# Layer 1's projections cut into half tiles and placed at the end of the attention rounds, their evacuation and splits one round later

## The chip, the cores and the metric

The kernel runs on one core of one Trainium2 chip. The metric is the device time of one execution in microseconds. Five engines work side by side: PE (matmuls), DVE (vector), ACT (activations, copies), POOL (GpSimd) and SP, which issues the transfers. Each has its own queue of instructions and waits for the others by semaphores.

## The reference

A two-layer transformer on 256 latent and 256 context tokens of width 1024, all in float32. Layer 0 mixes by window and latent attention, layer 1, the last, by differential attention of the latent tokens over all 512 tokens; each is followed by a mixture of experts (32 experts, two per token). The change touches layer 1's mixer:

```
h = modulate(rmsnorm(x), shift, scale)              # latent 256 x 1024, context 256 x 1024
q, k, v = split(h @ w_in, (1024, 1024, 1024))        # 8 heads; q, k: 2 x 64 each, v: 128
q1, q2, k1, k2 = rope(...)                           # of the latent tokens
lam = exp(lq1 . lk1) - exp(lq2 . lk2) + lambda_init
o = softmax(q1 k1' / 8) v - lam * softmax(q2 k2' / 8) v
x_lat = x_lat + gate * (rmsnorm(o, subln) * (1 - lambda_init)) @ w_out
```

## The kernel before

The program is recorded in the order in which it is written (manual_schedule, line 128), and each engine keeps that order. SBUF holds 24 buffers of 1 MB (S(), line 136), shared by data ("data") and by weights on their way ("w"). All weights come as a stream of 1 MB tiles in the order of plan(): emit() issues the next one on SP, pump() does so while fewer than 24 - max(budget, data) buffers hold weights, and budget(n) sets that bound. The expert weights of layer 1 follow behind layer 1's other weights in the same stream.

Matmuls that need more than single fp32r accuracy are done in three: mm3 (line 396) multiplies hi x hi, hi x lo and lo x hi. So each weight tile is split into hi and lo first: Splits.step (line 410) splits one half of 128 columns, a copy to hi on ACT or on another engine and a subtraction to lo, by default on DVE; get() hands out a finished tile and makes the next one, both halves.

w_in of layer 1 has 12 tiles of 256 columns: numbers 0 to 3 are q, 4 to 7 k, 8 to 11 v, in the order DWO. After the first (k, through proj_step) a loop runs the 11 others: k_tile and q_tile make two blocks of 128 rows of 24 matmuls each, of 512 columns for k (all tokens) and of 256 for q; v_tile makes two pieces of 48 matmuls of 256 columns, which read both halves of the tile. A q or k block is evacuated by rope_lat on DVE (line 565: one product, four products of 32 rows, one sum) and split again, hi on ACT and lo on POOL; a v piece is copied by ACT.

Then run_units goes through 16 units (8 heads x 2 blocks of 128 queries). Round i has, in this order: d_scores (6 matmuls) and d_max (DVE) of unit i + 2, the hook early1(i), d_pv of unit i - 1, a fill (a step of the modulation projections, 4 matmuls) in some rounds, d_scale (DVE) of unit i + 1, d_transpose of unit i (PE, copy on ACT), d_exp of unit i + 2 (ACT). The hook also splits half tiles of w_out in rounds 7, 9, 11 and 13, with both steps on POOL. Behind the rounds stand the turns of the outputs, the output projection (out_block) and the MoE of layer 1.

PSUM has four banks of tag A (scores), three of tag B (pieces, transposes, d_pv) and one of tag C (fills).

Of the kernel before, what the change touches and what calls it, by code (L numbers as in the profile page):

```python
# [19 lines left out]
P = 128  # L20
# [28 lines left out]

ADL = 3  # L50

DWO = (4, 5, 6, 8, 0, 7, 9, 1, 10, 2, 11, 3)
ADO = {0: (0, 1), 1: (2, 3, 4), 2: (5,), 3: (6,), 4: (7,)}

# [61 lines left out]
def model_kernel(ctx: ExitStack, tc: tile.TileContext, xin, small, cst, ada0, adaw, win, wuq, wukv, wout0, dwin,  # L116
# [24 lines left out]
    def free(n):  # L141
        st_["data"] -= n
# [41 lines left out]
    def U(shape=(512,), dt=F32):  # L184
        return up.tile([P] + list(shape), dt, tag="u", name="u")
# [7 lines left out]
    def psB():  # L193
        return psb.tile([P, 512], F32, tag="B", name="psB")
# [268 lines left out]
    def xc(c):  # L463
        return xmap[c]
# [44 lines left out]
    def h_lo(l, c, xa, hi, lo, gp=False):  # L509
        for s in range(2):  # L510
            hs, b = HALF[s], modT[:, l, 0, c, s:s + 1]
            if s and gp:
                GP.tensor_scalar(xa[:, hs], xa[:, hs], b, None, op0=ALU.add)
                GP.tensor_tensor(lo[:, hs], xa[:, hs], hi[:, hs].bitcast(F32), ALU.subtract)
            else:
                DVE.scalar_tensor_tensor(out=lo[:, hs], in0=xa[:, hs], scalar=b, in1=hi[:, hs].bitcast(F32),
                                         op0=ALU.add, op1=ALU.subtract)
# [44 lines left out]
    DVE.tensor_copy(UB, csv("U"))  # L562


    def rope_lat(ps, dst, p0, cosn, sinn):

        t = U((SEQ,))
        r = U((SEQ,))
        DVE.tensor_tensor(t[p0:P], ps[p0:P, 0:SEQ], csv(cosn)[p0:P], ALU.mult)
        for q in range(p0 // 32, 4):  # L570
            a, b = slice(32 * q, 32 * q + 32), slice(32 * (q ^ 1), 32 * (q ^ 1) + 32)
            DVE.tensor_tensor(r[b], ps[a, 0:SEQ], csv(sinn)[a], ALU.mult)  # L572
        DVE.tensor_tensor(dst[p0:P, 0:SEQ], t[p0:P], r[p0:P], ALU.add)
# [221 lines left out]
    def run_units(units, scores, maxs, exps, scale, transpose, pv, fills, hook, prime=0, ex=None):  # L795

        n = len(units)
        mx, pts, PT = {}, {}, {}
        if ex is None:
            ex = {}  # L800
            for i in range(2):
                ex[i] = exps(units[i], *maxs(units[i], scores(units[i])))
        fill(prime)
        pts[0] = scale(units[0], ex.pop(0))
        for i in range(n - 1):
            if i + 2 < n:
# [855 lines left out]
    for c in range(KC):  # L1662
# [13 lines left out]
    DVE.tensor_scalar(nlam, lamt[:, 2:3], -LAMBDA_INIT, None, op0=ALU.add)  # L1676
    k1 = [[S((4, NTOK), F32R) for _ in range(2)] for _ in range(2)]

    def k_out(j, ps):
        dst = U()  # L1680
        ACT.copy(dst[:, SEQ:], ps[:, SEQ:])
        rope_lat(ps, dst, 0, "cosA", "sinA")
        split(*(x[j // 4].v[:, j % 4, :] for x in k1), dst, GP)

    def k_tile(j2):
        ws = W1.get()
        for j in range(2):
            ps = psB()
            s = slice(j * P, (j + 1) * P)
            mm3(ps, KC, lambda k: (ws[0][:, k, s], ws[1][:, k, s]), h13)  # L1690
            k_out(2 * j2 + j, ps)
        free(2)

    def q_tile(j2):
        ws = W1.get()
        for j in range(2):
            ps = psB()
            s = slice(j * P, (j + 1) * P)
            mm3(ps[:, 0:SEQ], KC, lambda k: (ws[0][:, k, s], ws[1][:, k, s]),
                lambda k: tuple(x[:, 0:SEQ] for x in h13(k)))  # L1700
            dst = U((SEQ,))
            rope_lat(ps, dst, 0, "cosA", "sinA")
            split(*(x.v[:, 2 * j2 + j, :] for x in q1), dst, GP)
        free(2)

    def v_tile(j):
        ws = W1.get()
        for t2 in range(2):
            ps = psB()
            for t in range(2):  # L1710
                ts_ = slice((2 * t2 + t) * P, (2 * t2 + t + 1) * P)
                mm3(ps[:, t * 256:(t + 1) * 256], KC, lambda k: tuple(x[:, ts_] for x in h13(k)),
                    lambda k: (ws[0][:, k, :], ws[1][:, k, :]))
            ACT.copy(v1[j // 2].v[:, 2 * t2:2 * t2 + 2, (j % 2) * 256:(j % 2 + 1) * 256],
                     ps.rearrange("p (t n) -> p t n", t=2))
        free(2)

    wl = [W1.get(False)]
    pss = [psA() for _ in range(2)]
# [5 lines left out]
    free(2)  # L1725
    q1 = [S((KC, SEQ), F32R) for _ in range(2)]
    v1 = [S((4, 512)), S((4, 512))]
    budget(18)
    for j in DWO[1:]:
        (q_tile, k_tile, v_tile)[j // 4](j % 4)  # L1730
    free(4)
    oD = S((16, P))
    budget(11)

    def d_scores(u):
        h, qt = u
        ps = [psA(), psA()]
        for a, b in ((0, 0), (0, 1), (1, 0)):
            for i in range(2):
                pr = slice(64 * i, 64 * i + 64)  # L1740
                PE.matmul(ps[i], q1[a].v[pr, h, qt * P:(qt + 1) * P], k1[b][h // 4].v[pr, h % 4, :],
                          start=(a + b == 0), stop=(a == 1))
        return ps

    def d_max(u, ps):
        st = T((8,))
        for i in range(2):
            DVE.tensor_reduce(out=st[:, i:i + 1], in_=ps[i], axis=AX.X, op=ALU.max)  # L1748
        DVE.tensor_scalar(st[:, 2:4], st[:, 0:2], -0.125, None, op0=ALU.mult)
        return ps, st  # L1750
# [29 lines left out]
    def d_pv(u, PTs):  # L1780
        h, qt = u
        PT, rec = PTs
        ps = psB()
        for b in range(4):
            PE.matmul(ps[:, 0:P], PT[:, b * P:(b + 1) * P], v1[h // 4].v[:, b, (h % 4) * P:(h % 4 + 1) * P],
                      start=(b == 0), stop=(b == 3))
        sq = U((P,))
        ACT.activation(sq, ps[:, 0:P], AF.Square, scale=rec, accum_out=ssD[:, 0, 2 * h + qt:2 * h + qt + 1])
        DVE.tensor_scalar(oD.v[:, 2 * h + qt, :], ps[:, 0:P], rec, None, op0=ALU.mult)

# [18 lines left out]
        DVE.scalar_tensor_tensor(out=lo, in0=ps, scalar=sl1, in1=hi.bitcast(F32), op0=ALU.mult, op1=ALU.subtract)  # L1809

    def early1(i):
        if i in {2: 13, 10: 14}:
            budget({2: 13, 10: 14}[i])
        if i == 9:
            free(3)
            budget({2: 13, 10: 14}[10])
        if i in (7, 9, 11, 13):
            Wo.step(GP, GP)
        if i == 14:

            oDs.extend(S((KC, SEQ), F32R) for _ in range(2))
            d_rstd(0, 12)
        if i == 15:
            d_norm(0)
            d_norm(1)
            d_turn(0)
        if i == 16:
            d_norm(2)
            d_turn(1)

    run_units([(h, qt) for h in range(8) for qt in range(2)], d_scores, d_max, d_exp, d_scale, d_transpose, d_pv,
              lambda i: i in (1, 2, 3, 14, 15), early1, 3)
    d_rstd(12, 16)
    d_norm(3)
    d_turn(2)
# [196 lines left out]
```

## Time and profile before

| | us |
|---|---|
| runs: lowest, median, highest of three | 1467.99, 1470.62, 1471.46 |
| profiled execution, its own time | 1473.68 |
| its span, first to last instruction | 1471.9 |
| PE, DVE, ACT, POOL busy in the span | 1306.0, 578.9, 373.1, 139.6 |

The span is divided by what the program does: layer 1's projections begin with the first tile at 782 us, the other 11 run from 795.1 to 897.5, the attention rounds and their tail to 964.7, the output projection and the router to about 1017, and the MoE of layer 1 to the end. A matmul's end is modelled and neighbours overlap, so a busy PE is read together with the distance between starts.

### The profile page before, as it was taken

To read this page: it belongs to the slowest core of one execution; us is meant where nothing else is said; L and a number is where in the kernel's file an instruction comes from. 1 tells how busy PE (TensorE), PEld (TensorE's weight loads), DVE (VectorE), ACT (ScalarE), POOL (GpSimd) and SP (SyncE) were. 2 spreads that over 40 slices of the span, in tenths; PEclk is the share of its full clock that TensorE was granted. 3 is DMA by queue.
4 is the path that set the end of the run, shared out by engine and by line. 5 is a ranking of instruction groups with operands and counts; after the bars stand their busy time and mean duration, and the time that the engine had idled before them with its cause. 6 is when DMAs were issued, how large, how long until landed. Compare 5 with 4: busy or idle time off the path is not lost.

```text
span 1471.9 us, 21790 instructions
## 1 busy us (share of the span) xinstructions
PE 1306.0 (89%) x8439; PEld 720.9 (49%) x8439; DVE 578.9 (39%) x1423; ACT 373.1 (25%) x800; POOL 139.6 (9%) x129
## 2 busy tenths in 40 slices
PE   5998999989999989989889999797998786877867
PEld 3675668935435343525226896593432321323313
DVE  4577874464232313222237657945311110111102
ACT  4444654331111111101024334743110100101002
POOL 1112341210000000000013211211000000000000
PEclk9999999999999999999999999999999999999989
DMA  9834444489999999999998238356999999999995
GB/s 379 334 114 144 173 143 173 162 333 369 409 421 421 420 421 421 422 420 421 401 410 343 72 115 318 154 210 275 422 420 421 420 422 421 421 421 421 422 413 218
DMA packets 70076, 487.16 MB, mean 331 GB/s; under 512 B 7632, under 2 KB 7760, under 8 KB 13392
## 3 DMA queue, kind: packets, MB, share of 16 engines
q1 hardware_dynamic: 69968, 485.71, 81.2%
q8 instruction: 69, 1.13, 0.3%
q14 instruction: 39, 0.32, 0.1%
HBM read 484.63 MB, written 1.05 MB: 330 GB/s over the span
## 4 chain that ended last, share of the span: by engine, by line
DMA 26%; PE 16%; DVE 7%; ACT 2%; issue 1%; DVEq 0%; SPq 0%; ACTq 0%
DMA s<-in_ew_dram 26%; PE psA L1356 3%; PE psA L1388 2%; PE psB L402 2%; PE psB L403 2%; PE psB L401 2%; DVE t L1748 1%; DVE u L1766 1%; PE psA L401 1%; PE psA L402 1%; PE psA L403 1%; DVE s L394 1%; DVE u L572 0%; DVE t L1764 0%; DVE s L1398 0%
## 5 line engine op out<-in xcount | busy, mean ns | idle before, releaser
L1356 PE MATMUL psA<-s 128*32 128x512 f32 (+2 forms) x2336 | 420.9, 627 | 81.4 <-DMA s<-in_ew_dram 72.1
L1356 PEld LDWEIGHTS psA<-s 128*32 128x32 f32 (+2 forms) x2336 | 114.7, 122 | 364.2 <-issue 209.8
L1398 DVE SCALAR_TENSOR_TENSOR s<-psB,modT,s 128x256 f32<-128x256 f32 x296 | 120.4, 476 | 220.8 <-PE psB L1405 220.7
L1388 PE MATMUL psA<-s,u 128*32 128x512 f32 (+1 forms) x1168 | 186.9, 606 | 11.7 <-DMA s<-in_ew_dram 10.4
L1393 DVE SCALAR_TENSOR_TENSOR u<-psA,t,u 128x512 fp32r<-128x512 f32 x48 | 36.0, 750 | 232.5 <-ACT u L1392 232.5
L1388 PEld LDWEIGHTS psA<-s,u 128*32 128x32 f32 (+1 forms) x1168 | 54.5, 120 | 121.8 <-issue 95.2
L1405 PE MATMUL psB<-u 128*128 128x512 f32 (+1 forms) x384 | 95.8, 369 | 13.1 <-DVE s L1398 4.7
L1530 DVE TENSOR_TENSOR u<-u,psA 128x512 f32<-128x512 f32 x24 | 16.5, 688 | 221.6 <-PE psA L1356 221.6
L401 PE MATMUL psB<-s 128*128 128x256 f32 (+1 forms) x304 | 98.8, 325 | 0.2 <-DVE s L888 0.2
L402 PE MATMUL psB<-s 128*128 128x256 f32 (+1 forms) x304 | 98.1, 323 | 0.3 <-DVE s L394 0.3
L403 PE MATMUL psB<-s 128*128 128x256 f32 (+1 forms) x304 | 98.0, 322 | 0.0
L1382 ACT COPY u<-psB 128x512 f32<-128x512 f32 x24 | 14.1, 587 | 329.7 <-PE psB L1380 329.7
L1405 PEld LDWEIGHTS psB<-u 128*128 128x128 f32 x384 | 58.7, 188 | 72.4 <-issue 36.1
L1392 ACT ACTIVATE u<-psA,t 128x512 fp32r<-128x512 f32 x48 | 33.0, 688 | 176.6 <-PE psA L1388 171.1
L1527 ACT ACTIVATE u<-psA 128x512 f32<-128x512 f32 x24 | 14.4, 599 | 226.0 <-PE psA L1356 225.9
L1339 PE MATMUL psB<-s 128*128 128x256 f32 x544 | 68.0, 285 | 0.7 <-ACT u L1382 0.7
L394 DVE TENSOR_TENSOR s<-s 128x1024 fp32r<-128x1024 f32 (+3 forms) x56 | 51.6, 966 | 39.9 <-ACT s L391 39.9
L1339 PEld LDWEIGHTS psB<-s 128*128 128x128 f32 x544 | 65.9, 191 | 2.6 <-issue 1.6
L401 PEld LDWEIGHTS psB<-s 128*128 128x128 f32 x304 | 57.9, 190 | 8.4 <-issue 1.7
L402 PEld LDWEIGHTS psB<-s 128*128 128x128 f32 x304 | 57.9, 190 | 4.7 <-DVE s L394 0.6
L403 PEld LDWEIGHTS psB<-s 128*128 128x128 f32 x304 | 57.9, 190 | 4.5
L401 PE MATMUL psA<-s 128*128 128x256 f32 (+1 forms) x200 | 58.7, 294 | 0.0
(354 smaller groups left out, 1704.6 us busy)
## 6 DMA issues: line engine op xcount, KB each, us to landing
s<-in_ew_dram SPq DMA_DIRECT2D x376, 1024.0 KB, 19.8
s<-in_adaw_dram SPq DMA_DIRECT2D x40, 1024.0 KB, 6.8
s<-in_dwin_dram SPq DMA_DIRECT2D x12, 1024.0 KB, 9.8
s<-in_ada_dram SPq DMA_DIRECT2D x8, 1024.0 KB, 20.1
s<-in_wout_dram SPq DMA_DIRECT2D x8, 1024.0 KB, 8.3
s<-in_ew_dram SPq DMA_DIRECT2D x16, 512.0 KB, 15.3
s<-in_win_dram SPq DMA_DIRECT2D x5, 1024.0 KB, 21.1
s<-in_xin_dram SPq DMA_DIRECT2D x2, 1024.0 KB, 8.5
```

Of the source, the lines that this page charges most:

```text
L394: eng.tensor_tensor(lo, src, hi.bitcast(F32), ALU.subtract)
L401: PE.matmul(ps, lh, rh, start=(k == 0), stop=False)
L402: PE.matmul(ps, lh, rl, start=False, stop=False)
L403: PE.matmul(ps, ll, rh, start=False, stop=(k == n - 1))
L1339: PE.matmul(ps[:, i * n:(i + 1) * n], src(t, cs_(c0 + i)), oh[:, t, 0:n], start=(t == 0 and a == 0), stop=(t == T_ - 1 and a == 1))
L1356: PE.matmul(ps[sl, :], xg(hf * 4 + k, sl), wt(m, hf)[:, k, :], start=(hf == 0 and k == 0), stop=(hf == 1 and k == 3))
L1388: PE.matmul(ps[sl, :], ht[:, k, sl], wt(2, hf)[:, k, :], start=(k == 0), stop=(k == 3))
L1392: ACT.activation(yh, ps, AF.Copy, scale=gsl)
L1393: DVE.scalar_tensor_tensor(out=yl, in0=ps, scalar=gsl, in1=yh.bitcast(F32), op0=ALU.mult, op1=ALU.subtract)
L1398: DVE.scalar_tensor_tensor(out=xc(c)[:, HALF[s]], in0=ps[:, HALF[s]], scalar=modT[:, l, 5, c, s:s + 1], in1=xc(c)[:, HALF[s]], op0=ALU.mul ...
L1405: PE.matmul(ps[:, 0:nt], ysp[a][:, cs_(q)], oht[:, 0:nt], start=(a == 0), stop=(a == 1))
L1530: TT(hm, sl, pm[1], ALU.mult)
```

## The change

The tiles stand in another order (DWO; ADO holds the tiles of the modulation that go between them). The 11 tiles after the first are cut into 22 pieces, half a tile each. q_piece, k_piece and v_piece issue the matmuls at once and hand back two functions, one that evacuates and one that splits. Two pieces of q0 come ahead of everything, one of k1 behind the scores of each of the first two units, two of q1 ahead of round 0; the 16 others stand at the end of rounds, as PIECES lists. A round begins with evacs() (the pieces of the round before), and splits() stands behind its exponentials: per piece its split and, if no finished weight tile is there, one half of the next weight tile, with the subtraction on POOL. The temporaries of the rope and q's destination lie in the context halves of xT, which nothing reads any more. The three fills ahead of the rounds go into them, the splits of w_out go to rounds 12 to 15, and budget is 19 until round 9, where it was 18 and then 11.

```diff
-DWO = (4, 5, 6, 8, 0, 7, 9, 1, 10, 2, 11, 3)
+PIECES = {0: 2, 1: 1, 2: 1, 3: 1, 4: 2, 5: 2, 6: 1, 7: 1, 8: 2, 9: 1, 10: 1, 12: 1}
+DWO = (4, 0, 5, 1, 8, 9, 6, 2, 10, 7, 3, 11)
...
+    budget(19)
...
+    def q_piece(j2, j, ws):
+        ps = psB()
+        s = slice(j * P, (j + 1) * P)
+        mm3(ps[:, 0:SEQ], KC, lambda k: (ws[0][:, k, s], ws[1][:, k, s]),
+            lambda k: tuple(x[:, 0:SEQ] for x in h13(k)))
+        dst = room()
+        tr = (room(), room())
+        return (lambda: rope_lat(ps, dst, 0, "cosA", "sinA", tr),
+                lambda: split(*(x.v[:, 2 * j2 + j, :] for x in q1), dst, GP))
...
+    def piece(n=1):
+        for _ in range(n):
+            j, i = pieces.pop(0)
+            if i == 0:
+                cur.append(W1.get(False))
+            made.append((q_piece, k_piece, v_piece)[j // 4](j % 4, i, cur[0]))
...
+    def splits():
+        for n in range(len(made)):
+            made.pop(0)[1]()
+            if not W1.made:
+                W1.step(GP)
...
-    for j in DWO[1:]:
-        (q_tile, k_tile, v_tile)[j // 4](j % 4)
...
-    run_units([(h, qt) for h in range(8) for qt in range(2)], d_scores, d_max, d_exp, d_scale, d_transpose, d_pv,
-              lambda i: i in (1, 2, 3, 14, 15), early1, 3)
+    piece(2)
+    evacs()
+    splits()
+    for i in range(2):
+        mx1[i] = d_max(units[i], d_scores(units[i]))
+        piece()
+        ex1[i] = d_exp(units[i], *mx1.pop(i))
+    evacs()
+    pts1[0] = d_scale(units[0], ex1.pop(0))
+    splits()
+    piece(2)
+    for i in range(n_u + 1):
+        evacs()
+        if i + 2 < n_u:
+            mx1[i + 2] = d_max(units[i + 2], d_scores(units[i + 2]))
+        early1(i)
+        if 0 < i:
+            d_pv(units[i - 1], PT1.pop(i - 1))
+        if i in (2, 6, 11, 13, 14, 15):
+            fill()
+        if i + 1 < n_u:
+            pts1[i + 1] = d_scale(units[i + 1], ex1.pop(i + 1))
+        if i < n_u:
+            PT1[i] = d_transpose(units[i], pts1.pop(i))
+        if i + 2 < n_u:
+            ex1[i + 2] = d_exp(units[i + 2], *mx1.pop(i + 2))
+        splits()
+        if i in (12, 13, 14, 15):
+            Wo.step(GP, GP)
+        piece(PIECES.get(i, 0))
```

POOL from layer 1's norm (the first row) to the output weights, before. A subtraction of 128x512 or 128x256 is the split of a k or q block; 128x8x128 is half a weight tile.

```order
L514 TENSOR_TENSOR s<-u,s 128x256
L394 TENSOR_TENSOR s<-u,s 128x512 x6
L394 TENSOR_TENSOR s<-u,s 128x256 x2
L394 TENSOR_TENSOR s<-u,s 128x512 x2
L394 TENSOR_TENSOR s<-u,s 128x256 x6
L393 CAST s<-s 128x8x128
L394 TENSOR_TENSOR s<-s 128x8x128
```

The same place now, from the norm to the first of the long run of weight halves behind round 0:

```order
L516 TENSOR_TENSOR s<-u,s 128x256
L396 TENSOR_TENSOR s<-u,s 128x512 x2
L396 TENSOR_TENSOR s<-s 128x256
L396 TENSOR_TENSOR s<-s 128x8x128
L396 TENSOR_TENSOR s<-s 128x256
L396 TENSOR_TENSOR s<-s 128x8x128
L396 TENSOR_TENSOR s<-u,s 128x512
L396 TENSOR_TENSOR s<-s 128x8x128
L396 TENSOR_TENSOR s<-u,s 128x512
L396 TENSOR_TENSOR s<-s 128x8x128
L396 TENSOR_TENSOR s<-s 128x256
L396 TENSOR_TENSOR s<-s 128x8x128
```

Between the splits of the blocks POOL now has the weight halves: two of k1 (between q0's blocks), two of q1 (between k1's), two of v0 (between q1's), and so on, 18 in all.

ACT around the projection of k's third and v's first tile before, where L391 on u is the split of a block, L391 on s that of half a weight tile, and L1714 the copy of a v piece:

```order
L391 CAST s<-u 128x512
L391 CAST s<-s 128x8x128 x2
L1714 COPY s<-psB 128x2x256 x2
L391 CAST s<-s 128x8x128 x2
L391 CAST s<-u 128x256 x2
L391 CAST s<-s 128x8x128 x2
```

ACT in rounds 0 and 1 now (L1808 is the copy of the transposes, L1789 an exponential, L1728 the copy of a v piece, L1821 the square in d_pv, L393 a split):

```order
L1808 COPY u<-psB 128x512
L1789 ACTIVATE u,t<-psA,t 128x512 x2
L393 CAST s<-s 128x256
L393 CAST s<-s 128x8x128
L393 CAST s<-s 128x256
L393 CAST s<-s 128x8x128
L1728 COPY s<-psB 128x2x256 x2
L1821 ACTIVATE s,ssD<-psB,t 128x128
L1808 COPY u<-psB 128x512
L1789 ACTIVATE u,t<-psA,t 128x512 x2
L393 CAST s<-s 128x8x128 x2
```

The two casts of v0's weights stand behind the exponentials of round 0, and those of v1's behind the ones of round 1; PE has the pieces that read them at the end of the same rounds.

## Rows read from the trace of the kernel before

**Rows 1.** Busy time by stage: window, length, engines with instructions, PEclk, DMA share, GB/s

```profile
795.10:897.50 102.40, 102.09 (x721) 96.06 (x719) 63.66 (x112) 33.00 (x50) 14.81 (x14) 1.00 0.35 124
897.50:953.90 56.40, 47.41 (x326) 30.16 (x325) 53.08 (x114) 37.73 (x108) 15.75 (x10) 0.97 0.61 241
...
1000.00:1017.00 17.00, 10.26 (x51) 5.64 (x45) 11.72 (x43) 6.02 (x10) 3.65 (x4) 0.80 0.48 202
1017.00:1471.90 454.90, 369.59 (x2115) 139.03 (x2115) 77.91 (x217) 50.72 (x90) 1.90 (x1) 0.96 0.97 402
```

**Rows 2.** Order of time, PE, projections: start, length, line and operation

```profile
795.09 0.39 PE L401 MATMUL psB<-s 128*128 128x512 f32 x1
...
795.54 0.40 PE L403 MATMUL psB<-s 128*128 128x512 f32 x1
...
897.20 0.28 PE L402 MATMUL psB<-s 128*128 128x256 f32 x1
897.32 0.28 PE L403 MATMUL psB<-s 128*128 128x256 f32 x1
```

**Rows 3.** Order of time, PE, one attention round

```profile
939.44 0.63 PE L1773 MATMUL psB<-identR,u 128*128 128x128 f32 x4 [0.16 <-DVE u L1766]
940.00 0.96 PE L1741 MATMUL psA<-s 64*128 64x512 f32 x6
940.89 1.16 PE L1785 MATMUL psB<-s,u 128*128 128x128 f32 x8
```

**Rows 4.** Order of time, DVE: a rope, and the maxima of a round

```profile
799.81 0.42 DVE L569 TENSOR_TENSOR u<-psA,u 128x256 f32<-128x256 f32 x1 [1.00 <-ACT u L1681]
800.25 1.72 DVE L572 TENSOR_TENSOR u<-psA,u 32x256 f32<-32x256 f32 x4
802.00 0.42 DVE L573 TENSOR_TENSOR u<-u 128x256 f32<-128x256 f32 x1
...
939.21 1.28 DVE L1748 TENSOR_REDUCE t<-psA 128x1 f32<-128x512 f32 x2
```

**Rows 5.** Order of time, ACT: from an exponential to what follows the second

```profile
938.02 0.69 ACT L1756 ACTIVATE u<-psA,t 128x512 f32<-128x512 f32 x1
...
939.36 0.36 ACT L1788 ACTIVATE u<-psB,t 128x128 f32<-128x128 f32 x1
```

**Rows 6.** Groups by line, 796 to 898 us: busy, mean ns, idle before

```profile
L394 DVE TENSOR_TENSOR s<-s 128x1024 fp32r<-128x1024 f32 x21 | 25.8, 1267 | 25.2 <-ACT s L391 25.2
...
L391 ACT CAST s<-s 128x1024 fp32r<-128x1024 f32 x20 | 20.0, 1047 | 0.0
...
L394 POOL TENSOR_TENSOR s<-u,s 128x512 fp32r<-128x512 f32 x8 | 10.4, 1297 | 33.1 <-ACT s L391 33.1
...
L394 POOL TENSOR_TENSOR s<-u,s 128x256 fp32r<-128x256 f32 x7 | 5.2, 740 | 56.3 <-ACT s L391 56.3
L391 ACT CAST s<-u 128x512 fp32r<-128x512 f32 x8 | 5.0, 620 | 27.2 <-DVE u L573 23.4 <-issue 3.8
...
L391 ACT CAST s<-u 128x256 fp32r<-128x256 f32 x7 | 2.8, 406 | 24.1 <-DVE u L573 24.1
```

**Rows 7.** Order of time, DVE and POOL: one operation alone, and beside a weight half

```profile
903.56 0.22 DVE L1764 SCALAR_TENSOR_TENSOR t<-t,nlam 128x1 f32<-128x1 f32 x1
...
916.02 2.42 DVE L1764 SCALAR_TENSOR_TENSOR t<-t,nlam 128x1 f32<-128x1 f32 x1
...
916.06 2.37 POOL L394 TENSOR_TENSOR s<-s 128x1024 fp32r<-128x1024 f32 x1 [2.60 <-PE psC L323]
```

**Rows 8.** Order of time, PE, the round behind its longest wait

```profile
926.31 0.88 PE L1773 MATMUL psB<-identR,u 128*128 128x128 f32 x4 [3.66 <-DVE u L1766]
927.12 1.65 PE L1741 MATMUL psA<-s 64*128 64x512 f32 x6
928.70 1.77 PE L1785 MATMUL psB<-s,u 128*128 128x128 f32 x8
```

**Rows 9.** Busy time, two microseconds of that round, columns as in group 1

```profile
928.00:930.00 2.00, 2.00 (x10) 1.35 (x9) 1.97 (x4) 0.28 (x1) 1.60 (x1) 0.50 0.00 0
```

More of the change, by code (lines that the diff above doesn't have):

```diff
@@ L50 @@
 ADL = 3
-DWO = (4, 5, 6, 8, 0, 7, 9, 1, 10, 2, 11, 3)
-ADO = {0: (0, 1), 1: (2, 3, 4), 2: (5,), 3: (6,), 4: (7,)}
+PIECES = {0: 2, 1: 1, 2: 1, 3: 1, 4: 2, 5: 2, 6: 1, 7: 1, 8: 2, 9: 1, 10: 1, 12: 1}
+DWO = (4, 0, 5, 1, 8, 9, 6, 2, 10, 7, 3, 11)
+ADO = {0: (0, 1), 1: (2, 3, 4), 6: (5,), 9: (6,), 11: (7,)}
 NFIX = (4, 4)
@@ L562, in model_kernel, with rope_lat @@
     DVE.tensor_copy(UB, csv("U"))
-    def rope_lat(ps, dst, p0, cosn, sinn):
-        t = U((SEQ,))
-        r = U((SEQ,))
+    def rope_lat(ps, dst, p0, cosn, sinn, tr=None):
+        t, r = tr or (U((SEQ,)), U((SEQ,)))
         DVE.tensor_tensor(t[p0:P], ps[p0:P, 0:SEQ], csv(cosn)[p0:P], ALU.mult)
@@ L1677, in model_kernel, with room, k_rope, k_split @@
     k1 = [[S((4, NTOK), F32R) for _ in range(2)] for _ in range(2)]
+    rooms_ = [0]
+    def room():
+        rooms_[0] += 1
+        return xc(rooms_[0] % KC)[:, SEQ:]
+    def k_rope(dst, ps):
+        ACT.copy(dst[:, SEQ:], ps[:, SEQ:])
+        rope_lat(ps, dst, 0, "cosA", "sinA", (room(), room()))
     def k_out(j, ps):
         dst = U()
-        ACT.copy(dst[:, SEQ:], ps[:, SEQ:])
-        rope_lat(ps, dst, 0, "cosA", "sinA")
+        k_rope(dst, ps)
+        k_split(j, dst)
+    def k_split(j, dst):
@@ L1683, in k_out @@
         split(*(x[j // 4].v[:, j % 4, :] for x in k1), dst, GP)
[L1685 to L1716, printed above, removed]
+    def k_piece(j2, j, ws):
+        ps = psB()
+        s = slice(j * P, (j + 1) * P)
+        mm3(ps, KC, lambda k: (ws[0][:, k, s], ws[1][:, k, s]), h13)
+        dst = []
+        def evac():
+            dst.append(U())
+            k_rope(dst[0], ps)
+        return evac, lambda: k_split(2 * j2 + j, dst[0])
@@ new lines, in q_piece, with v_piece @@
+    def q_piece(j2, j, ws):
+        ps = psB()
+        s = slice(j * P, (j + 1) * P)
+        mm3(ps[:, 0:SEQ], KC, lambda k: (ws[0][:, k, s], ws[1][:, k, s]),
[4 more added lines that the diff above has]
+                lambda: split(*(x.v[:, 2 * j2 + j, :] for x in q1), dst, GP))
+    def v_piece(j, t2, ws):
+        ps = psB()
+        for t in range(2):
+            ts_ = slice((2 * t2 + t) * P, (2 * t2 + t + 1) * P)
+            mm3(ps[:, t * 256:(t + 1) * 256], KC, lambda k: tuple(x[:, ts_] for x in h13(k)),
+                lambda k: (ws[0][:, k, :], ws[1][:, k, :]))
+        return (lambda: ACT.copy(v1[j // 2].v[:, 2 * t2:2 * t2 + 2, (j % 2) * 256:(j % 2 + 1) * 256],
+                                 ps.rearrange("p (t n) -> p t n", t=2)), lambda: None)
@@ new lines, in model_kernel, with evacs @@
+    pieces = [(j, n) for j in DWO[1:] for n in range(2)]
+    cur, made = [], []
+    def piece(n=1):
[4 more added lines that the diff above has]
+            made.append((q_piece, k_piece, v_piece)[j // 4](j % 4, i, cur[0]))
+            if i:
+                cur.pop()
+                free(2)
+    def evacs():
+        for e, _ in made:
+            e()
+    def splits():
[3 more added lines that the diff above has]
+                W1.step(GP)
@@ L1727, in model_kernel @@
     v1 = [S((4, 512)), S((4, 512))]
-    budget(18)
-    for j in DWO[1:]:
-        (q_tile, k_tile, v_tile)[j // 4](j % 4)
-    free(4)
     oD = S((16, P))
-    budget(11)
     def d_scores(u):
@@ L1786, in d_pv @@
                       start=(b == 0), stop=(b == 3))
-        sq = U((P,))
+        sq = room()[:, 0:P]
         ACT.activation(sq, ps[:, 0:P], AF.Square, scale=rec, accum_out=ssD[:, 0, 2 * h + qt:2 * h + qt + 1])
@@ L1811, in early1 @@
     def early1(i):
-        if i in {2: 13, 10: 14}:
-            budget({2: 13, 10: 14}[i])
         if i == 9:
             free(3)
-            budget({2: 13, 10: 14}[10])
-        if i in (7, 9, 11, 13):
-            Wo.step(GP, GP)
+            budget(16)
+        if i == 14:
+            free(4)
+            budget(14)
         if i == 14:
@@ L1829, in early1 @@
             d_turn(1)
-    run_units([(h, qt) for h in range(8) for qt in range(2)], d_scores, d_max, d_exp, d_scale, d_transpose, d_pv,
-              lambda i: i in (1, 2, 3, 14, 15), early1, 3)
+    units = [(h, qt) for h in range(8) for qt in range(2)]
+    n_u, ex1, mx1, pts1, PT1 = len(units), {}, {}, {}, {}
+    piece(2)
[28 more added lines that the diff above has]
+        piece(PIECES.get(i, 0))
     d_rstd(12, 16)
```

## Prediction

> **What bounds the kernel now.** I read the busy time of the engines by stage first, then the order of time on each engine, then groups of instructions by line for their durations. From 795.1 to 897.5 us the projections keep PE busy for 102.1 of 102.4 us; from 897.5 to 953.9 the attention rounds leave PE idle for 56.4 - 47.4 = 9.0 us while DVE is busy for 53.1 [rows 1]. So PE sets the first of these stages, and DVE the second. Behind them comes the MoE of layer 1, where the DMA share is 0.97 for 455 us [rows 1]. Its weights can be fetched ahead only into the 24 buffers, and in the 17 us before it the DMA share is 0.48: the buffers are full and wait for the program. A microsecond gained or lost ahead of 1000 us therefore reaches the end whole, and I count the change by when PE begins the output projection (964.7 us before).
>
> Prices of PE work. Matmuls of 512 columns start 0.225 us apart (0.45 from the first to the third), those of 256 columns 0.12 us [rows 2]. A half tile of q (24 of 256) is 2.9 us, of k (24 of 512) 5.4, of v (48 of 256) 5.75. A round's own work is transposes 0.56, scores 0.89 and products with v about 1.1 us, 2.6 in all [rows 3]. DVE needs 2.6 us for one rope and 1.28 for the two maxima [rows 4], 1.45 with their scaling (two columns, a little less than the 0.22 of one such operation in [rows 7]); ACT 1.35 for two exponentials [rows 5], 1.05 for the cast of half a weight tile, 0.6 for a k block's, 0.4 for a q block's [rows 6]. The subtraction of a split costs POOL 1.3 us for a k block, 0.74 for q [rows 6], and 2.37 for half a weight tile [rows 7], where DVE took 1.27 before, contention with POOL included [rows 6].
>
> **The change, part by part.** PE's work stays the same: 11 tiles are cut into 22 pieces, and three fills move from ahead of the rounds into them. What it can gain is the idle time of the rounds, 9.0 us, and the time lost to the lower clock behind the gap at 922.7 to 926.3: transposes 0.88 for 0.63, scores 1.65 for 0.96, products 1.77 for 1.16, together 1.5 [rows 3, 8]. **Removed: 10.5 us.**
>
> What it adds is a wait. Before, a weight tile was split on DVE a whole tile ahead (get() makes the next one). Now its two halves are split by ACT and POOL at the end of a round, behind that round's exponentials on ACT and behind the split of the round's own pieces on POOL, and the piece that reads them stands at the end of the same round, or of the next. PE has only 2.6 us of its own in between. A v piece reads all 256 columns, so both halves. Place by place (the instants are worked out from the prices):
>
> 1. *q0, k1, q1, ahead of the rounds.* PE ends q0 at 795.1 + 48 x 0.12 = 800.9. DVE ends k0's second rope at 802.4 [rows 4]; q0a's rope brings 805.0, ACT's cast 805.4, POOL's subtraction 806.2, and only then do the first scores end; k1's first half follows with cast and 2.37 on POOL at 808.9. PE has 1.4 us of work up to there and waits 6.6. Then k1a, scores, k1b to 820.2. For q1 ACT copies and casts k1's two blocks first: cast of k1a at 821.3, POOL 1.3 + 2.4 to 825.2, a wait of 5.0; its second half comes 1.0 after q1a. **12.6 us.**
> 2. *Round 0, v0.* From the end of q1b: rope 2.6, maxima 1.45, exponentials 1.35, cast 0.4, that is 5.8; then POOL, for which the casts come in time, 0.74 + 2.37 + 0.74 + 2.37 = 6.2, with the handing over 12.1. PE has scores and transposes, 1.5. **10.6 us.**
> 3. *Round 1, v1.* Transposes end at 2.6, their copy and the exponentials on ACT at 4.55, cast 5.6, POOL twice 10.3; PE's own 2.6. **7.7 us.**
> 4. *Rounds 4 and 8, q2a and q3a.* rope, maxima, exponentials, cast, POOL 1.3 + 2.37: 9.7; PE's own 2.6 and a k piece, 8.0. **3.3 us** for both.
> 5. *Round 5, v2.* rope (behind k2b's) 3.5, maxima 4.95, exponentials 6.3, cast 6.9, POOL 1.3 + 2.37 + 0.74 + 2.37 = 13.8; PE's own 2.6 and a q piece 2.9. **8.3 us.**
> 6. *Round 10, scores of head 6.* They need q3a's split from the end of round 9: 6.9 + 1.3 + 2.37 + 0.74 = 11.3 behind the round's start, against 5.5; 0.4 more for v3. **5.8 us.**
> 7. *Rounds 11 and 12.* The four output-weight splits on POOL (moved from rounds 7 to 13 to 12 to 15) hold up DVE as before; one v piece covers a part. **2.7 us.**
>
> The pieces of rounds 2, 3, 6, 7, 9 and 12 have their weights from a round earlier and wait for nothing. Sum of the added waits 51.0 us. DVE's own step of q2 and q3 (1.1 us each) is inside 4; the v copies on ACT (0.6) lie beside the scores; the temporaries that move into the unused halves of xT change no shape. On SP the order of the weight tiles changes, with 5 buffers for them where 6 to 13 were free. Each tile is asked for more than a round (8 us) ahead; and at the end the same 10 buffers are allowed, two of them still held by modulation weights: 2 x 2.6 us (1.05 MB at 402 GB/s) against 8.8 us of idle DMA ahead of the MoE [rows 1]. I cost it at nothing; without that cover 5 us.
>
> The clock: after the 3.66 us wait at 926 PE ran at 0.50 of full speed, the lower level of 1.2 GHz [rows 8, 9], and lost 1.5 us until it was back. Six of the new waits are as long or longer (1 twice, 2, 3, 5, 6). Taken: 6 x 1.5 = 9.0 us; bounds 0, if work resumes gently, and 18, twice that, as the dense matmuls that follow here lose half of every microsecond at that clock. The Trainium skill, "TensorE: Matmul & The Clock Gate", section "HAM oscillation — how this bites in real kernels", says that a loop whose bursts are parted by waits pays the cold start at every one of them. By that rule all six pay, as taken; the trace shows it for the one gap.
>
> A lock between DVE and POOL: while POOL subtracted from 916.06 to 918.43, DVE's one-column operation on SBUF took 2.42 us, where 0.22 is usual, and ended with it [rows 7]. I have counted this for DVE in 7 alone. The Trainium skill, "SBUF — State Buffer", section "SBUF: two separate sides", says that whichever of the two starts first has the shared port for its whole instruction, so POOL would also wait for DVE. By it some twelve POOL subtractions on the path would each wait up to 0.75 us (DVE's scaling), and the sum would be up to 9 higher; by the row alone it stays. That is in the upper end.
>
> Sum: 51.0 + 9.0 - 10.5 = **+49.5 us**. The profiled execution took 1473.7, so 1523 for one like it; the median of the three runs is 3.1 lower, and the prediction 1470.6 + 49.5 = **1520 us**. Bounds: low, no clock cost and none of the waits under 3.5 us (4, 7, second parts of 1 and 6): 51.0 - 7.4 - 10.5 = +33, or 1504; high, clock 18 and lock 9: +67.5, or 1538.
>
> **The rivals.**
> - *The splits are covered after all (faster).* If ACT and POOL had each half tile ready before PE came to it, only the removed 10.5 us would count: 1460. It decides in round 0: the chain of 12.1 us behind q1b would have to be shorter than PE's 1.5. For it: POOL is busy for 15.8 of 56.4 us in the rounds now [rows 1], so it has room. Against it: the order of the queues, where the casts stand behind the exponentials and each half behind the other. Chance 0.05. The Trainium skill, "Perfetto Trace Analysis", section "Optimizing Scalar/DVE Operations", holds that breaking up instructions may let work end sooner where other engines cause bubbles, which is this rival's hope; here the pieces end sooner but their weights do not.
> - *Gains and waits cancel.* That needs the waits at 10.5 in place of 51; the one at v0 alone is that long. 0.03.
> - *Only the four long waits stand* (2, 3, 5 and 5.4 of 6, 32.0 us with 4 x 1.5 of clock): +27.5, or 1498. For it: the start and the k rounds have slack on DVE that my chains may not use. Against: in the trace every engine takes its instructions in program order, and the ropes stand ahead of the maxima. 0.12.
> - *The output weights come late.* They follow the last modulation weights in the stream and are first asked for in round 9, when three buffers come free; eight tiles take 8 x 2.6 = 21 us, against some 25 us to round 12. If half of them miss it, 10 us on top, and the upper bounds of clock or lock with it: 1545. Against it: the rounds are slow, which gives the transfers time. 0.10.
>
> **How the numbers follow.** The forecast has 0.70. A difference of 0.3% (4.4 us) is about what a measurement of this kernel can tell from none. Faster by more: the first rival, 0.05. Within it: 0.03. Slower: 0.92. The range takes the bounds of the sum and the third rival, widened by some hops between engines that I priced at 0.1 us or nothing: 1492 to 1542, which leaves out 0.05 + 0.03 + 0.10.
>
> **What would show it.** Right: in the changed profile PE waits for POOL ahead of the first matmuls of v0, v1 and v2 for 8 to 11 us each, and for POOL ahead of the scores of head 6; POOL busy for some 73 us from 795 us to the output projection (18 half tiles x 2.37, 16 k and q blocks, output weights 14); the granted clock falls to 0.5 after each of these waits; the output projection begins near 1014 us, and the MoE's stretch keeps its 455 us. Wrong: PE at 95% or more from 800 to 950 us, or the waits there ending on DVE or a DMA in place of POOL; or a MoE stretch that is shorter because the weights had more time to come.

## The result, and the profile after

| | before | changed |
|---|---|---|
| median of 4 runs, us | 1471.04 | 1522.31 |
| lowest to highest, us | 1467.99 to 1472.56 | 1519.85 to 1525.33 |
| profiled execution, its own time / span, us | 1473.68 / 1471.9 | 1525.33 / 1523.5 |
| PE begins the output projection, us | 964.67 | 1016.57 |

The ratio is 1.0345, with an interval from 1.0328 to 1.0362: the change costs 51.3 us in the medians. The prediction was 1520 us. The profiled executions differ by 51.65 us, and the start of the output projection by 51.9, so all of it is lost ahead of the output projection, and nothing comes back behind it.

Busy time of the engines in the stretch from the second weight tile to the output projection, of the kernel before (columns as in [rows 1]):

```profile
795.10:964.70 169.60, 156.76 (x1090) 132.65 (x1088) 124.09 (x244) 76.78 (x171) 30.56 (x24) 0.98 0.46 173
```

and of the changed kernel, with its MoE stretch below, which answers to the last of [rows 1]:

```profile
795.60:1016.60 221.00, 172.50 (x1090) 144.06 (x1088) 108.59 (x224) 76.72 (x172) 72.12 (x42) 0.88 0.31 114
1068.00:1523.50 455.50, 375.43 (x2123) 140.38 (x2119) 79.08 (x223) 50.72 (x90) 1.90 (x1) 0.94 0.97 401
```

The same work, 1090 matmuls in either trace, takes 221.0 us in place of 169.6. PE's idle time grew from 169.60 - 156.76 = 12.8 to 48.5 us, and its busy time from 156.8 to 172.5, at a mean granted clock of 0.88 where it was 0.98. So the loss has two parts: **35.7 us more of waiting and 15.7 us of slower matmuls.** DVE gave up 15.5 us of work, POOL took 41.6 more. The MoE has its 455 us and its 0.97 of DMA share, as before.

What PE waits for, from the view of waits grouped by the instruction that released it (total, times, longest), before:

```profile
PE psB L1773 <- DVE u L1766: 9.6, 12, 3.7
```

and after:

```profile
PE psB L403 <- ACT s L393: 15.7, 4, 6.8
PE psB L404 <- POOL s L396: 10.9, 3, 4.0
PE psA L1774 <- ACT s L393: 6.8, 2, 4.7
PE psB L405 <- POOL s L396: 6.0, 4, 2.2
PE psA L1774 <- POOL s L396: 2.4, 1, 2.4
...
PE psB L403 <- DVE s L573: 1.7, 4, 0.5
PE psB L1806 <- DVE u L1799: 1.3, 2, 0.8
```

The waits of the transposes for DVE's scaling, 9.6 us, shrank to 1.3: that part of the change works. In their place stand waits of the projection matmuls (L403 to L405, the three of mm3) and of the scores (L1774) for the casts (L393, ACT) and the subtractions (L396, POOL) of split(). No wait of PE in this stretch ends on a DMA, and none of DVE, ACT or POOL does.

One of these places in full, v0 (v's first tile) in round 0, from the orders of time of DVE, ACT, POOL and PE (start, length):

```profile
837.87 0.42 DVE L574 TENSOR_TENSOR s<-s 128x256 f32<-128x256 f32 x1
838.32 1.29 DVE L1781 TENSOR_REDUCE t<-psA 128x1 f32<-128x512 f32 x2
...
840.59 0.68 ACT L1789 ACTIVATE u<-psA,t 128x512 f32<-128x512 f32 x1
...
841.25 2.60 ACT L393 CAST s<-s 128x256 fp32r<-128x256 f32 x4
...
841.73 0.72 POOL L396 TENSOR_TENSOR s<-s 128x256 fp32r<-128x256 f32 x1 [9.46 <-ACT s L393]
842.67 5.33 POOL L396 TENSOR_TENSOR s<-s 128x1024 fp32r<-128x1024 f32 x3 [0.22 <-ACT s L393]
...
843.90 0.58 PE L403 MATMUL psB<-s 128*128 128x256 f32 x1 [6.78 <-ACT s L393]
848.05 0.58 PE L404 MATMUL psB<-s 128*128 128x256 f32 x1 [3.57 <-POOL s L396]
848.43 0.41 PE L405 MATMUL psB<-s 128*128 128x256 f32 x1
848.65 0.41 PE L403 MATMUL psB<-s 128*128 128x256 f32 x1
...
853.64 0.28 PE L403 MATMUL psB<-s 128*128 128x256 f32 x1
853.75 0.28 PE L404 MATMUL psB<-s 128*128 128x256 f32 x1
```

The chain reads downwards: the rope of q1's second block ends at 838.3, the maxima at 839.6, the exponentials at 841.3, the four casts at 843.9, the last subtraction at 848.0. PE stops twice, 6.78 us for ACT and 3.57 for POOL: the first matmul of a v piece is hi x hi and needs the casts alone, the second (L404) takes the weight's lo and needs the subtraction. In a k or q piece the weight's lo comes with the third (L405), so there the wait for POOL stands ahead of L405. Then the matmuls start 0.213 us apart, and 0.12 only from 853.6 on. The granted clock behind the long waits shows the same (windows, columns as in [rows 1]):

```profile
806.00:812.00 6.00, 5.21 (x14) 3.21 (x15) 5.19 (x9) 3.08 (x6) 4.54 (x4) 0.50 0.00 1
824.00:833.00 9.00, 6.06 (x28) 5.86 (x29) 5.03 (x9) 2.26 (x3) 7.20 (x4) 0.62 0.00 1
848.00:852.00 4.00, 3.95 (x18) 3.95 (x19) 0.00 (x0) 0.00 (x0) 0.00 (x0) 0.50 0.00 0
872.00:879.00 7.00, 6.78 (x38) 6.78 (x39) 0.00 (x0) 0.00 (x0) 0.17 (x1) 0.62 0.00 0
907.00:912.00 5.00, 4.06 (x31) 3.52 (x32) 4.87 (x9) 0.00 (x0) 0.89 (x1) 1.00 0.37 116
924.00:930.00 6.00, 5.66 (x32) 5.67 (x33) 0.57 (x1) 0.00 (x0) 0.28 (x1) 0.62 0.58 178
960.00:963.00 3.00, 3.00 (x25) 2.78 (x26) 2.91 (x7) 0.00 (x0) 0.00 (x0) 1.00 0.54 229
970.00:978.00 8.00, 5.02 (x22) 4.14 (x23) 4.16 (x10) 2.58 (x7) 5.98 (x4) 0.68 0.60 250
```

Six of the eight have the lower level, 1.2 GHz, in them: the start (806), q1 (824), v0, v1, v2 and head 6 (970). The other two, behind the waits of 1.61 and 1.63 us ahead of the first halves of q's third and fourth tile (q2a at 907, q3a at 960), stay at 1.00.

### The profile page after: what moved, and what is told of

The parts are those of the page before. It is cut to its first block, busy times and chain, and to the rows that moved or that the text cites. A ratio compares the mean times of both kernels' runs of the same rounds, so it can differ in the third digit from the quotient of the medians.

```text
span 1523.5 us, 21791 instructions
## 1 busy us (share of the span) xinstructions
PE 1324.3 (87%) x8439; PEld 733.5 (48%) x8439; DVE 563.7 (37%) x1405; ACT 373.1 (24%) x800; POOL 181.1 (12%) x147
## 3 DMA queue, kind: packets, MB, share of 16 engines
HBM read 484.63 MB, written 1.05 MB: 319 GB/s over the span
## 5 line engine op out<-in xcount | busy, mean ns | idle before, releaser
L403 PE MATMUL psB<-s 128*128 128x256 f32 (+1 forms) x304 | 105.9, 348 | 17.6 <-ACT s L393 15.7
L404 PE MATMUL psB<-s 128*128 128x256 f32 (+1 forms) x304 | 103.8, 341 | 10.9 <-POOL s L396 10.9
L405 PE MATMUL psB<-s 128*128 128x256 f32 (+1 forms) x304 | 103.6, 341 | 6.0 <-POOL s L396 6.0
L396 POOL TENSOR_TENSOR s<-s 128x1024 fp32r<-128x1024 f32 (+2 forms) x39 | 77.7, 2002 | 141.4 <-ACT s L393 105.0
L1406 PEld LDWEIGHTS psB<-u 128*128 128x128 f32 x384 | 58.7, 188 | 72.0 <-issue 35.7
L403 PEld LDWEIGHTS psB<-s 128*128 128x128 f32 x304 | 63.3, 208 | 28.5 <-ACT s L393 16.8
L404 PEld LDWEIGHTS psB<-s 128*128 128x128 f32 x304 | 63.1, 208 | 15.8 <-POOL s L396 11.7
L405 PEld LDWEIGHTS psB<-s 128*128 128x128 f32 x304 | 63.1, 208 | 12.0 <-POOL s L396 7.4
L1340 PEld LDWEIGHTS psB<-s 128*128 128x128 f32 x544 | 65.9, 191 | 2.6 <-issue 1.6
L1630 POOL TENSOR_TENSOR u<-u 128x256 f32<-128x256 f32 x8 | 5.6, 733 | 461.8 <-PE psB L1406 458.1
```

The lines of the kernel that those rows point to most:

```text
L1340: PE.matmul(ps[:, i * n:(i + 1) * n], src(t, cs_(c0 + i)), oh[:, t, 0:n], start=(t == 0 and a == 0), stop=(t == T_ - 1 and a == 1))
L1406: PE.matmul(ps[:, 0:nt], ysp[a][:, cs_(q)], oht[:, 0:nt], start=(a == 0), stop=(a == 1))
```

## The experiments

**The theory**: each weight half is split just in time, at the end of the round, and PE waits for the end of that chain and then runs at the lower clock. **Rivals**: POOL is too slow for this work wherever it stands; or the interleaving itself (ropes ahead of the maxima, pieces among the rounds) costs the time. The first four runs cross the two things that the change altered for the splits, their place and their engine, and take the splits away. Where a stretch counts, I give the start of the output projection beside the time. The profiled executions come into the stage at different instants, though: PE starts the second weight tile between 793.6 and 796.2 us (795.09 in the kernel before, 795.57 in the changed one). So the length of the stage, from that matmul to the output projection, is given too: 169.6 us before, 221.0 changed.

**A tile ahead, on POOL** (ahead_pool)

```diff
     cur.append(W1.get(False))
+    W1.step(GP)
+    W1.step(GP)
...
     made.pop(0)[1]()
-    if not W1.made:
-        W1.step(GP)
```

> The two halves of a weight tile are split where the tile before it is taken, a whole tile ahead, with the subtraction still on POOL. Theory (the splits come just in time): the waits of PE ahead of q1, v0, v1, v2, q2a, q3a and head 6 go (2.2 + 10.4 + 7.2 + 7.1 + 3.2 + about 3.5 of 4.4 us) and with them most of the 15.7 us of lower clock; 1480 us, between 1468 and 1492; PE busy above 90% from 825 us to the output projection. Rival (POOL's price and its hold on DVE, wherever the split stands): POOL stays at 72 us busy and the time at 1512 or more. Rival (the interleaving itself, ropes and pieces among the rounds): waits of PE on DVE take the place of those on POOL, 1505 or more.

Measured: 1484.85 us (1480.15 to 1490.81), 1.0072 of the kernel before, from 1.0045 to 1.0099; the output projection begins at 978.0, and the stage takes 184.2. Only the place of the splits moved, and 37.5 of the 51.3 us are gone. POOL is as busy as ever (77.72 us from 795.3 to 978.0), so its work as such is not what these 37.5 us paid for.

**At the end of the round, on DVE** (jit_dve)

```diff
-    W1.step(GP)
+    W1.step()
```

> The splits stay at the end of the round, the subtraction goes from POOL back to DVE. Theory (the place is at fault, not the engine): each wait only gets shorter by the difference of the two prices, about 1.1 us per half tile, 2.2 for a v tile, some 10 us in all, the ACT part (15.7 us ahead of first matmuls) stays; 1512 us, between 1503 and 1520. Rival (POOL's price): most of the loss goes, 1485 or less.

Measured: 1512.48 us (1510.21 to 1513.05); the output projection begins at 1004.5, stage 210.9. Ahead of v0 PE now shows:

```profile
843.94 0.58 PE L403 MATMUL psB<-s 128*128 128x256 f32 x1 [6.78 <-ACT s L393]
845.62 0.58 PE L404 MATMUL psB<-s 128*128 128x256 f32 x1 [1.10 <-DVE s L396]
```

The wait for ACT is the same 6.78 us, and the second part fell from 3.57 to 1.10. A faster engine shortens the tail of the chain and leaves its head. I had expected every wait to get shorter, but q1's second one grew from 2.20 to 4.08 us. The rival of POOL's price wanted 1485 or less.

**A tile ahead, on DVE** (ahead_dve): as the first, with the subtractions of both halves on DVE (the casts stay on ACT).

> A whole tile ahead and on DVE, as the kernel before splits, with the pieces still in the rounds. Theory (place): within 6 us of the version a tile ahead on POOL, so about 1480 us (1468 to 1492); DVE has 22 halves of about 1.1 us more and POOL some 43 us less. Rival (POOL's price): clearly below that version, by 15 us or more. Rival (interleaving itself): 1505 or more.

Measured: 1477.93 us (1476.02 to 1485.08), 1.0049, from 1.0030 to 1.0068; output projection at 969.4, stage 175.0. The place is worth 37.5 us on POOL and 34.6 on DVE; the engine 9.8 us at the end of the round and 6.9 a tile ahead. So the place is the larger cause in either case, and POOL a smaller one of its own. The longest wait left is at the start, where the scores need q0's split behind k0's ropes and k1's subtractions:

```profile
PE psA L1774 <- ACT s L393: 10.2, 2, 9.0
```

**No weight splits at all** (no_split)

```diff
-    cur.append(W1.get(False))
+    if j != DWO[1]:
+        use(("dwin", j))
+        freew(1)
+    cur.append(old[0])
...
-    if not W1.made:
-        W1.step(GP)
...
     free(2)
+    old.append(W1.get(False))
...
```

> No weight tile after q0's is split at all: every later piece reads q0's two buffers, and the other ten tiles are fetched and given up unread, so that the products are those of the wrong weights. What is left is the interleaving with its ropes, block splits and rounds. Theory (splits just in time): all that hangs on weights goes, the output projection begins at about 960 to 970 us and the time is 1465 us (1455 to 1480). Rival (the interleaving itself costs): 1500 or more.

Measured: 1512.20 us (1510.10 to 1518.35), and the output projection at 964.4. The two disagree, and the time is not the number to read. This kernel leaves out most weights of the projection, so other products reach the choice of experts: this run fetches 490.92 MB from HBM where the kernel before and the changed one fetch 484.63, and one expert's weights are waited for 18.3 us near the end:

```profile
PE psA L1469 <- DMA s<-in_ew_dram: 22.7, 3, 18.3
```

Behind the start of the output projection it takes 546.9 us where the kernel before takes 507.2. At the 401 GB/s of the MoE the 6.3 MB are 16 us of these 40, an estimate; the others are not taken apart. My expectation of 1465 us missed that; it should have been made for the stage alone. There the theory's 960 to 970 held. It also shows what the interleaving can give: with no weight split at all the stage takes 796.1 to 964.4, 168.3 us, and the kernel before needed 169.6 with them. PE's waits still come to some 12.6 us in it, 4.7 of them at the start.

**Matmuls in PE's pauses** (warm): the lower clock by itself.

```diff
     def v_piece(j, t2, ws):
         ps = psB()
+        for _ in range({0: 40, 1: 27, 2: 27}.get(j, 0) if t2 == 0 else 0):
+            PE.matmul(ps, hhi[0].v[:, 0, 0:P], hhi[0].v[:, 0, :], start=True, stop=True)
```

> The changed kernel with matmuls put ahead of the first piece of v0, v1 and v2 (40, 27 and 27 of 512 columns, on operands that are long there, into the bank that the piece then overwrites). They run while PE would wait for the splits, so nothing becomes ready earlier; only PE's pause is cut from 10.4, 7.2 and 7.1 us to about 1. Theory (a wait costs its length and then the lower clock): the pieces behind run at full clock from the start, about 2.3 us less at each place (24 matmuls of 256 columns 0.12 apart in place of 0.213), 7 us in all: 1515 us (1511 to 1519), the output projection near 1009.5. Rival (the lower clock is not a matter of PE's own pauses): 1520 to 1524. If the added work outlasts the waits: above 1524.

Measured: 1517.80 us (1515.90 to 1518.75), 4.5 below the changed kernel's median; the output projection begins at 1009.5, the forecast's instant and 7.1 earlier than in the changed kernel. Not all of that is due to the added matmuls: this execution came into the stage earlier (794.34 for 795.57), and at q1, ahead of the first added matmul, it was still 0.83 us ahead. PE at q1 in the changed kernel, then here:

```profile
824.75 0.39 PE L403 MATMUL psB<-s 128*128 128x256 f32 x1 [1.98 <-ACT s L393]
823.92 0.39 PE L403 MATMUL psB<-s 128*128 128x256 f32 x1 [1.98 <-ACT s L393]
```

So 6.3 us are left for the three places. In the same four microseconds behind v0's wait PE now starts twice as many matmuls, at full clock (beside 848 to 852 above):

```profile
848.00:852.00 4.00, 4.00 (x36) 4.00 (x35) 0.00 (x0) 0.00 (x0) 0.00 (x0) 1.00 0.01 4
```

94 matmuls more, and the kernel is faster. So the pauses themselves are what lowers the clock, and one of these three long waits costs about 6.3 / 3 = 2.1 us on top of its length. The times fell by less than the trace (4.5 in the medians, 7.4 between the profiled spans). The profiled execution of the changed kernel was the slowest of its four, 3.0 above their median, and the one here lies 0.3 above its own; what is left between 4.5 and 6.3 is not settled.

**Only the v tiles a tile ahead** (v_ahead): do the terms stand by themselves?

```diff
     cur.append(W1.get(False))
+    if pieces and any(p[0] // 4 == 2 and p[0] != j for p in pieces[1:2]):
+        W1.step(GP)
+        W1.step(GP)
```

> Of the changed kernel's splits only those of the v tiles are made a whole tile ahead (in the queue where the tile before is taken, still on POOL); q1, k2, q2, k3 and q3 stay at the end of their rounds. Theory (the terms of the sum stand each by itself): the waits ahead of v0, v1 and v2 go, 10.4 + 7.2 + 7.1 us, and their 7 us of lower clock, 31.6 us in all: 1491 us (1486 to 1497), with the waits at the start, ahead of q2a and q3a (3.2) and ahead of head 6 (4.4) as they were. Rival (a wait that goes only comes back at the next weight tile): 1505 or more.

Measured: 1488.30 us (1486.46 to 1491.88), 34.0 less than the changed kernel; output projection at 980.1, stage 185.9. The waits at the start and ahead of q2a and q3a stay as they were, those ahead of the scores of head 6 shrink:

```profile
PE psB L405 <- POOL s L396: 6.4, 5, 2.2
PE psA L1777 <- ACT s L393: 5.7, 2, 4.7
PE psB L403 <- ACT s L393: 2.0, 1, 2.0
```

(L1777 is the scores' line here.) Ahead of head 6 PE now waits 0.97 us for ACT and 1.00 for POOL, where it waited 2.08 and 2.36: POOL has no half of v3 (2.37 us) ahead of q3a's subtraction any more. My expectation kept these 4.4 us; the 2.5 that went are about what the time fell beyond its 31.6. The v tiles, four of the ten that are split late, carry two thirds of the loss, and their terms can be taken away almost alone.

**Towards a version that keeps the gain.** From ahead_dve, the start in another order (dense_start): k1's pieces directly behind k0, then q0 with q1's halves between the ropes, a fill (the one of round 2), both scores, q1.

```diff
-DWO = (4, 0, 5, 1, 8, 9, 6, 2, 10, 7, 3, 11)
+DWO = (4, 5, 0, 1, 8, 9, 6, 2, 10, 7, 3, 11)
...
     piece(2)
     evacs()
     splits()
+    piece(2, False)
+    for e, _ in made:
+        e()
+        W1.step()
+    splits()
+    fill()
     for i in range(2):
         mx1[i] = d_max(units[i], d_scores(units[i]))
-        piece()
+    piece(2)
...
```

> A whole tile ahead on DVE, with the start in another order: k1's two pieces right behind k0, then q0, a fill, the scores of the first two units, then q1's two pieces. Theory (what is left over the kernel before is the start's wait of 9.0 us for the chain k0 rope, k1's split, q0 rope, cast, subtraction): that wait falls to about 1 us, the output projection begins near 961 to 963 and the time is 1470 us (1464 to 1476), level with the kernel before or a little below. Rival (DVE has no room, the start's wait only moves on to q1 and v0): 1475 to 1480.

Measured: 1474.78 us (1470.48 to 1480.81), 1.0023, from 1.0010 to 1.0035. The output projection begins at 963.5, 1.2 us earlier than in the kernel before, and the stage takes 168.6 us, 0.9 less, yet the median is 3 us above it; the profiled execution, with a span of 1470.0, was one of the fastest of these runs, and where the others lose the 3 us no trace shows. The start's wait of 9.0 us became 2.07 + 0.55, where I expected 1:

```profile
815.20 0.73 PE L1774 MATMUL psA<-s 64*128 64x512 f32 x4 [2.07 <-ACT s L393]
816.48 1.29 PE L1774 MATMUL psA<-s 64*128 64x512 f32 x8 [0.55 <-POOL s L396]
```

From dense_start, with the pieces of rounds 3 to 8 moved so that q3a comes a round earlier (dense_start_early_q3):

```diff
-PIECES = {0: 2, 1: 1, 2: 1, 3: 1, 4: 2, 5: 2, 6: 1, 7: 1, 8: 2, 9: 1, 10: 1, 12: 1}
+PIECES = {0: 2, 1: 1, 2: 1, 3: 2, 4: 1, 5: 2, 6: 2, 7: 2, 8: 1, 10: 1, 12: 1}
```

> The same, and the pieces of rounds 3 to 8 moved so that q3a is split a round before the scores of head 6 (k3a to round 6, k3b and q3a to round 7, q3b to round 8). Theory: the 2.2 us of waits ahead of those scores go, and 1 us ahead of v2: 1467 us (1461 to 1473). Rival: DVE's ropes, now denser in rounds 4 to 8, hold up the maxima, and it is 2 us or more above the version without it.

Measured: 1476.70 us (1472.40 to 1482.13), 1.0032, from 1.0018 to 1.0046; output projection at 968.6, stage 174.4. A miss: the waits ahead of head 6 went, but the pieces taken out of later rounds no longer cover the scaling there, and a transpose waits for DVE as it did before the change:

```profile
930.02 0.66 PE L1806 MATMUL psB<-identR,u 128*128 128x128 f32 x4 [3.52 <-DVE u L1799]
```

From dense_start again, with a second fill at the start (the one of round 6) and q3a evacuated ahead of k3b (dense_start_q3_first):

```diff
-    fill()
+    fill(2)
...
     for i in range(n_u + 1):
+        if i == 9:
+            made.reverse()
         evacs()
...
```

> The version with the dense start, with a second fill ahead of the first scores (taken from round 6) and, in round 9, q3a evacuated and split before k3b. Theory: the 2.6 us ahead of the first scores and the 2.2 us ahead of head 6 go; the output projection begins near 959 and the time is 1470 us (1466 to 1475), not to be told from the kernel before. Rival (the waits move on to the next transposes): 1474 or more.

Measured: 1473.49 us (1468.94 to 1476.32), 1.0011, from 0.9998 to 1.0023; output projection at 964.5. That is later than without these two steps, but only because this execution came into the stage at 796.24 in place of 794.82: the stage takes 168.3 us, 0.3 less. I expected 4.8 us less, so it is a miss all the same: ahead of head 6 PE waits 2.01 us for ACT in one piece, where it waited 1.21 for ACT and 1.00 for POOL, and of the 2.07 + 0.55 at the start 1.21 + 0.55 are left. Its time can't be told from the kernel before. No version that I ran beats it.

## Why the prediction was right, and where its terms were off

The prediction held for the reasons that it gave, with two errors of opposite sign: the waits were put 8.7 us too high, the clock 8.2 too low. That 1520 came so close to 1522.3 is therefore partly luck. By its steps:

| step | predicted | in the trace |
|---|---|---|
| 1, ahead of the rounds | 12.6 | 4.74 + 0.58 + 1.98 + 2.20 = 9.5 |
| 2, v0 | 10.6 | 6.78 + 3.57 = 10.35 |
| 3, v1 | 7.7 | 3.90 + 3.25 = 7.15 |
| 4, q2a and q3a | 3.3 | 1.61 + 1.63 = 3.24 |
| 5, v2 | 8.3 | 3.03 + 4.05 = 7.08 |
| 6, head 6 | 5.8 | 2.08 + 2.36 = 4.44 |
| 7, output weights | 2.7 | 0.57 |
| sum of the waits | 51.0 | 42.3 |
| idle time removed | 9.0 | 8.3 (9.6 to 1.3) |
| clock, added less removed | 9.0 - 1.5 = 7.5 | 15.7 |
| in all | 49.5 | 49.7; the stage grew by 51.4 |

- **What the table leaves over**: the 0.57 of step 7 is among the 1.3 that are left of the waits for the scaling, so it stands twice, and some 2 us are short waits that the prediction did not have. Most of them are the four of 0.33 to 0.50 us of a k or q piece for a PSUM bank that a rope still reads (L403 <- DVE L573 above, 1.7 in all).
- **The sums as written**: step 6 gives 11.3 - 5.5 = 5.8 without the 0.4 for v3, and the third rival takes 5.4 of it for the same chain; the fourth rival's 1545 is reached neither with one upper bound (1539) nor with both (1548). The forecast hangs on none of these differences.
- **The chains (2 to 5)** came out within 1.3 us each: prices from rows of the kernel before, put together in the order of the queues, were enough.
- **The waits sum to 42.3 where I had 51.0**, and part of the difference is the clock under another name. At step 1 the half of k1 that ends the first wait is ready at 809.5 us (808.9 in the prediction), but PE's own work between q0 and that instant takes 2.8 us where I had 1.4: the scores and the first two matmuls of k1 run at the lower clock inside the time that I had counted as waiting. For the same reason PE comes later to q1 and finds less to wait for. Why steps 6 and 7 came out 1.4 and 2.1 lower I have not taken apart.
- **The clock** is the mis-sized term. I took 6 x 1.5 us by the one gap of [rows 8]; the number of places, six, was right, the price was not. The gap before was followed by short work of a round; here it is followed by dense matmuls, 25 of them 0.213 us apart in place of 0.12 at v0, 2.3 us. The three v places cost about 2.1 each by the run with matmuls in the pauses. Of the rest, 15.7 + 1.5 - 6.3 = 10.9 us, I have only the low clocks at the start, q1 and head 6, not a run. The upper bound of 18 that the prediction named was the nearer one.
- **What should show it**: POOL's busy time (73 predicted, 72.1), the output projection (1014, 1016.6) and the MoE's 455 us came as said. One sign was wrong: I expected PE to wait for POOL ahead of the first matmuls of v0, v1 and v2, 8 to 11 us. It waits for ACT there first, and for POOL one matmul later, because hi x hi needs no subtraction, and at v1 and v2 the two come to 7.1 us only. Of the two, ACT is the larger at v0 and v1.
- **The lock** between DVE and POOL: I counted it for DVE and put the other direction (POOL waits for DVE, up to 9 us) in the upper end. It was hardly needed: no subtraction of a weight half takes POOL more than 2.41 us (2.37 in [rows 7]), and the longest of a k block takes 1.48 where [rows 6] have a mean of 1.30.
- **The rivals**: "gains and waits cancel" falls by the wait at v0 alone, 10.35 us; "only the four long waits stand" falls, since 1 and 4 stand too; "the output weights come late" falls, since no wait of PE, DVE, ACT or POOL in the stretch ends on a DMA; "covered after all" fails where it was said to be decided, at v0. What it would have needed is a split a tile ahead, and even so the versions here only come back to the kernel before.

The Trainium skill, "TensorE: Matmul & The Clock Gate", section "HAM oscillation — how this bites in real kernels", was the rule by which every long wait pays the cold start. The trace agrees at six of eight places (granted clock 0.50 to 0.68 in those windows, 1.00 behind the two waits of 1.6 us).

## What to carry to other kernels

When work is moved between two stages to fill idle time, look at what its inputs hang on in the queue where they are made: here filling 9 us of idle time put a chain of rope, maxima, exponentials, cast and subtraction ahead of matmuls that had been ready a tile early. Price such a wait as its length plus the matmuls that then run at the lower clock, and take that from the work that follows it, not from a gap elsewhere. And make operands one tile ahead first: that was worth 34.6 to 37.5 us here, the choice of the engine 6.9 to 9.8.

## What the runs showed of the hardware

An addition on DVE with both inputs in SBUF (L574, the sum of a rope) stretches when POOL subtracts at the same time, and the products of the same rope, with one input in PSUM (L573), do not. In the changed kernel, DVE and POOL at 824 us:

```profile
823.77 1.72 DVE L573 TENSOR_TENSOR s<-psB,u 32x256 f32<-32x256 f32 x4
825.53 2.15 DVE L574 TENSOR_TENSOR u<-s 128x256 f32<-128x256 f32 x1
...
823.83 1.27 POOL L396 TENSOR_TENSOR s<-u,s 128x512 fp32r<-128x512 f32 x1 [10.15 <-ACT s L393]
825.05 2.34 POOL L396 TENSOR_TENSOR s<-s 128x1024 fp32r<-128x1024 f32 x1
```

The four products take 0.43 us each beside POOL; the sum takes 2.15 us and ends 0.29 us after POOL's. Over the whole stage the 56 products that read a PSUM bank of tag B take 421 ns each with the weight halves on POOL and on DVE alike; the sums do not. By groups, with the splits a tile ahead, first on POOL and then on DVE:

```profile
L574 DVE TENSOR_TENSOR s<-s 128x256 f32<-128x256 f32 x8 | 7.5, 934 | 0.3
L574 DVE TENSOR_TENSOR u<-s 128x256 f32<-128x256 f32 x8 | 6.7, 834 | 0.4
```

```profile
L574 DVE TENSOR_TENSOR s<-s 128x256 f32<-128x256 f32 x8 | 3.4, 426 | 0.3
L574 DVE TENSOR_TENSOR u<-s 128x256 f32<-128x256 f32 x8 | 3.4, 425 | 0.4
```

That is 7.4 us of DVE's time in one stage, and it is a part of what POOL costs where place is not at fault. The Trainium skill, "SBUF — State Buffer", section "Who interferes with whom", says that an instruction of DVE with two SBUF inputs contends with one of GpSimd that reads SBUF, and one with at most one such input does not, outside DVE's modes with two ports. These rows agree on both halves. It also fits [rows 7], whose one-column operation has two SBUF inputs too.

The second surprise is that the time of this kernel seems to depend on its data: in the one run with the products of other weights 6.3 MB more were read and the part behind the stage took 40 us longer, although the stage under study ended where it should. A run that leaves out arithmetic ahead of a router is read by its stage, not by its time.
